# Earlier loads for the gate stage, three units ahead of its norm, and the last products on VectorE alone

## The chip, the core and the metric

The kernel runs on one core of a Trainium2 chip. The metric is the device time of one execution in microseconds (us). The core has a matrix engine, TensorE (PE), which multiplies 128 x 128 weights into 512 columns at a time; VectorE (DVE) and ScalarE (ACT) for elementwise work; GpSimd (POOL), which here adds squares and issues some transfers; and SyncE (SP), whose queue issues nearly all transfers between the device memory and the core's own memory. Each engine runs its own list of instructions in order and waits on semaphores of the others.

## The reference

One decoder layer on 1024 tokens of 2048 features in fp32:

```
hn = rmsnorm(h);  proj = hn @ w_in              # q, k, v, gate of two groups of 8 heads
mixed = [stick_breaking(..) * silu(g1), rmsnorm(differential(..)) * silu(g2)]
h = h + mixed @ w_out                           # 2048 x 2048
gate = sigmoid(rmsnorm(h) @ w_ple_gate)         # 2048 x 2048
h = h + gate * (p @ w_ple_proj)                 # p has 256 features
return rmsnorm(h)
```

The change lies in the last three lines and in the passage from the output projection to them.

## The kernel before

All tensors are held transposed: features on the 128 partitions, tokens along the free axis. The 1024 tokens are worked in two halves of 512; half 1 goes first through every stage, then half 0. The 2048 features are 16 channels of 128, and channels u and u + 8 belong to "unit" u. Every fp32 product is made of three matmuls on a high and a low part of each operand (high x high, high x low, low x high). ScalarE casts the high part and VectorE subtracts it to get the low part. For the gate these are `whi` (L151) and `wlo` (L152), made from the loaded `wraw` by `wprep`; `whi`, `wlo` and `wraw` each have two buffers.

*Output projection.* It runs as seven products of half the size (`prod`, matmuls L756 to L758) in two phases of eight units. In the second phase each unit loads four pieces of the residual (`hr`, L948) and adds them on VectorE (L972, L993, L996 and L939); the sums `hc` are put into the device buffer `h_d` by an accumulating transfer that GpSimd's queue issues (L744). The last unit's S4 product writes into a PSUM half whose other half `hc` of L939 reads.

*Gate stage.* `gate_loads` (L910 to L914) reads `h_d` back and makes `xh` and `xl`, the operands of the gate. `embedding` (L655 to L657) loads the 256 features of p (`praw`) and makes `ph` and `pl`, of which there is one copy. `plew` (L665 to L669) loads and splits a unit's projection weights (`pw`), and `ple` (L677 to L681) is 12 matmuls and a copy by ScalarE to `pls`. The tiles `praw`, `pw` and `hr` share the ring "xt" of four buffers, so a load waits until the tile four places earlier has been read. A gate unit, `unit` (L213 to L215), is 96 matmuls in four chunks of 24, one set of weights a chunk.

*Norm of the gate.* Its sum of squares is made beside the first units: `load_h` reads `h_d`, ScalarE squares (L105, L109), GpSimd adds (L110). The function `rstd` (L122 and L90 to L94) sums over the partitions on PE and takes the power; it needs two switches of ScalarE's function table and a third for the sigmoid. The norm scales the accumulator only after the matmuls: `gated` (L689 to L692) multiplies `acc` by `rstd`, takes the sigmoid, multiplies by `pls` and adds to h. For half 1, before: ple 0, ple 1, unit 0, unit 1 with the norm's matmul ahead of its last chunk, then for u from 2 to 7 ple u and unit u. Then follows half 0 in the same manner, with the final norm of half 1 beside it.

*The end.* The last unit is made in two quarters of 256 tokens (`tq`, L1108 to L1122). The sum of squares of the final norm closes behind each, and `final` (L623, L626) multiplies h by it and sends it out (L633): for the first quarter on GpSimd, for the second three pairs on GpSimd and the rest on VectorE.

*Order of the work.* PE's list is written out by hand over the whole kernel. Those of VectorE and ScalarE are written out by hand only in the output projection (`man2`) up to the first gate unit; behind that a planner, which simulates the engines, sorts them, and it sorts GpSimd's and SP's lists too.

Of the kernel before, what the change touches and what calls it, by code (L numbers as in the profile page):

```python
# [13 lines left out]
F32 = mybir.dt.float32  # L14
# [32 lines left out]
def _body(ctx, nc, tc, ap):  # L47
# [96 lines left out]
    def wprep(wsrc, pc, by_halves=False):  # L144
        raw = wp.tile([P, 2, 2, 2, P], F32, name="wraw", tag="wraw", bufs=2)
        hi = wp.tile([P, 2, 2, 2, P], F32R, name="whi", tag="whi")
        lo = wp.tile([P, 2, 2, 2, P], F32R, name="wlo", tag="wlo")

        def part(o):
            lastw[0] = nc.sync.dma_start(raw[:, o], wsrc[pc][:, o])  # L150
            A.copy(hi[:, o], raw[:, o])  # L151
            V.tensor_tensor(lo[:, o], raw[:, o], hi[:, o].bitcast(F32), op=ALU.subtract)  # L152

        part(slice(0, 1 if by_halves else 2))
        return hi, lo, partial(part, slice(1, 2))

    class Stream:
# [11 lines left out]
        def prep(self, by_halves=False):  # L169
            hi, lo, second = wprep(*self.todo.popleft(), by_halves=by_halves)  # L170
            self.ready.append((hi, lo))
            return second
# [261 lines left out]
    with tc.tile_pool(name="at", bufs=2) as at, tc.tile_pool(name="pz", bufs=2, space=PSUM) as pz:  # L434
# [217 lines left out]
        def embedding(half):  # L652
            for k in range(2):
                praw = ev.tile([P, HALF], F32, name="praw", tag="xt", bufs=4)
                nc.sync.dma_start(praw, ap["pT"][k * P:(k + 1) * P, half * HALF:half * HALF + HALF])  # L655
                A.copy(ph[:, k, :], praw)
                V.tensor_tensor(pl[:, k, :], praw, ph[:, k, :].bitcast(F32), op=ALU.subtract)  # L657
# [4 lines left out]

        def plew(half, u):
            wr = ev.tile([P, 2, 2, P], F32, name="pw", tag="xt", bufs=4)
            nc.sync.dma_start(wr, ap["w_pp"][u])  # L665
            wh = at.tile([P, 2, 2, P], F32R, name="pwh", tag="awh")
            wl = at.tile([P, 2, 2, P], F32R, name="pwl", tag="awl")
            A.copy(wh, wr)
            V.tensor_tensor(wl, wr, wh.bitcast(F32), op=ALU.subtract)  # L669
            plws[half, u] = wh, wl  # L670

        def ple(half, u):
            wh, wl = plws.pop((half, u))
            z = pz.tile([P, 2, HALF], F32, name="ple", tag="z")
            for c in range(2):
                for k in range(2):
                    T.matmul(z[:, c, :], wh[:, k, c, :], ph[:, k, :], start=k == 0, stop=False)  # L677
                    T.matmul(z[:, c, :], wh[:, k, c, :], pl[:, k, :], start=False, stop=False)
                    T.matmul(z[:, c, :], wl[:, k, c, :], ph[:, k, :], start=False, stop=k == 1)
            pls = pair("pls", "st")  # L680
            A.copy(pls, z)  # L681
            plss[half, u] = pls
# [259 lines left out]
        for ph in range(2):  # L942
            for u in range(8):
                last = ph == 1 and u == 7
                r = {}
                for e in ((1, u), (1, u + 8), (0, u), (0, u + 8)) if ph else ():
                    r[e] = ev.tile([P, HALF], F32, name="hr", tag="xt", bufs=4)
                    nc.sync.dma_start(r[e], half_d[e])  # L948
# [17 lines left out]
                if ph:  # L966
                    V.tensor_tensor(u2, u2, r[1, u + 8], op=ALU.add)

# [28 lines left out]
                if last:  # L997
                    p2()
                prev = u, ph, b, c, s1, u2
# [14 lines left out]
        while xq and len(xq) > 8:  # L1014
            xq.popleft()[1]()
# [26 lines left out]
        gated(1, 0, acc0, rstd)  # L1042
        gated(1, 1, acc1, rstd)
        for u in range(2, 8):
# [54 lines left out]
        for tq in range(2):  # L1099
# [13 lines left out]
            for c in range(2):  # L1113
# [8 lines left out]
                T.matmul(ms, ones, s, start=False, stop=c == 1)  # L1122
            with tc.issue_after(sgi.ins):
# [63 lines left out]
```

## Time and profile before

| | before |
|---|---|
| runs, us | 2513.76, 2515.78, 2515.96 |
| median, us | 2515.78 |
| the profiled execution's own time, us | 2510.27 |
| its span, us | 2508.5 |
| TensorE's mean granted clock, of 1 | 0.992 |
| TensorE busy | 2441.4 us, 97% |
| VectorE, ScalarE, GpSimd busy | 67%, 46%, 12% |

All times inside the profile count from the start of the span. The profiled execution is itself 2510.27 us, 1.8 us more than its span, and 5.5 us under the median of the three runs, so a sum made from its rows is a difference to be carried over to the median. In a row of the time order the columns are start, duration, engine, line, operation, what it writes and reads, tile shape, and in brackets the idle time of that engine ahead of it with what released it. A row of the windows gives the stretch, its length, the busy time of PE, weight loads, VectorE, ScalarE and GpSimd with instruction counts, then the granted clock of PE, the share of the transfer engines and the rate. The gate stage of half 1 runs from about 2083 us to 2287, that of half 0 to about 2500.

### The profile page before, as it was taken

Reading aid. Unit: us, or ns where it says so; the run is one execution under the profiler, and the core shown is the slowest. Engines: PE = TensorE matmul, PEld = TensorE weight load, DVE = VectorE, ACT = ScalarE, POOL = GpSimd, SP = SyncE. Lnnn points to the kernel's source line nnn. Section 1 sums busy time; section 2 is a strip of 40 time slices with the busy share of each in tenths; the row PEclk is TensorE's granted clock in tenths of the full one; section 3 lists DMA queues with packets and bytes.
Section 4 is the critical chain, followed back from the end, with each engine's and each line's share of the span. In section 5 each row is a group of like instructions: output and inputs, shape, how many; then the busy total and the mean of one; then the engine's idle time right before and its main releaser. Section 6 shows DMA issues by size and latency. Waiting matters only on the chain.

```text
span 2508.5 us, 31234 instructions
## 1 busy us (share of the span) xinstructions
PE 2441.4 (97%) x11626; PEld 2034.8 (81%) x11626; DVE 1668.4 (67%) x2677; ACT 1161.9 (46%) x1920; POOL 288.9 (12%) x281
## 2 busy tenths in 40 slices
PE   8999999999999999999999999999999998999996
PEld 7888888788887888888887888887787876888886
DVE  6554555777877888888876565667678673547555
ACT  6332333555556655555555333335523224637342
POOL 3000000300000000001111010101021114321112
PEclk9999999999999999999999999999999999999998
DMA  5333333633334333334443333435656786333433
GB/s 189 113 116 116 114 105 125 206 123 118 109 122 164 121 107 122 114 117 143 148 142 126 101 126 94 135 113 183 228 190 217 164 199 211 129 119 115 133 101 101
DMA packets 135415, 346.26 MB, mean 138 GB/s; under 512 B 14496, under 2 KB 18592, under 8 KB 135264
## 3 DMA queue, kind: packets, MB, share of 16 engines
q1 hardware_dynamic: 114096, 288.43, 35.6%
q0 software_dynamic: 21168, 55.85, 7.8%
q8 instruction: 91, 1.49, 0.2%
q14 instruction: 60, 0.49, 0.1%
HBM read 281.31 MB, written 71.30 MB: 141 GB/s over the span
## 4 chain that ended last, share of the span: by engine, by line
PE 87%; DVE 7%; DMA 2%; ACT 2%; issue 1%; SPq 0%; DVEq 0%; ACTq 0%
PE acc L213 20%; PE acc L214 20%; PE acc L215 20%; PE tp L345 2%; PE pbc L756 2%; PE pbc L758 2%; PE pbc L757 2%; DVE st L306 1%; PE z L286 1%; PE z L287 1%; PE av L378 1%; DVE wlo L152 1%; PE av L377 1%; PE av L376 1%; PE pa L758 1%
## 5 line engine op out<-in xcount | busy, mean ns | idle before, releaser
L213 PE MATMUL acc<-xh,whi 128*128 128x512 f32 x2464 | 981.4, 398 | 6.3 <-ACT xh L138 6.3
L214 PE MATMUL acc<-xl,whi 128*128 128x512 f32 x2464 | 963.9, 391 | 0.8 <-DVE xl L139 0.8
L215 PE MATMUL acc<-xh,wlo 128*128 128x512 f32 x2464 | 964.0, 391 | 0.0
L152 DVE TENSOR_TENSOR wlo<-wraw,whi 128x1024 fp32r<-128x1024 f32 (+1 forms) x317 | 398.8, 1258 | 374.5 <-ACT whi L151 369.2
L215 PEld LDWEIGHTS acc<-xh,wlo 128*128 128x128 f32 x2464 | 463.6, 188 | 101.1 <-DVE wlo L152 1.3
L151 ACT CAST whi<-wraw 128x1024 fp32r<-128x1024 f32 (+1 forms) x317 | 333.0, 1051 | 457.2 <-PE acc L214 397.0
L213 PEld LDWEIGHTS acc<-xh,whi 128*128 128x128 f32 x2464 | 464.8, 189 | 93.6 <-ACT xh L138 6.8
L214 PEld LDWEIGHTS acc<-xl,whi 128*128 128x128 f32 x2464 | 464.9, 189 | 88.3 <-DVE xl L139 2.3
L357 ACT CAST awh<-tp 128x256 fp32r<-128x256 f32 (+1 forms) x160 | 80.3, 502 | 180.9 <-PE tp L345 153.5
L358 DVE TENSOR_TENSOR awl<-tp,awh 128x256 fp32r<-128x256 f32 (+1 forms) x160 | 93.1, 582 | 97.9 <-ACT awh L357 96.7
L110 POOL TENSOR_TENSOR ssq<-ssq,sq 128x512 f32<-128x512 f32 x80 | 119.0, 1488 | 326.6 <-ACT sq L109 278.8
L314 ACT ACTIVATE et<-z,mx 128x512 f32<-128x512 f32 (+7 forms) x128 | 94.6, 739 | 53.6 <-DVE mx L311 52.7
L865 ACT CAST wpr<-T 128x512 fp32r<-128x512 f32 x64 | 39.2, 623 | 164.9 <-DVE T L822 164.0
L306 DVE TENSOR_TENSOR_SCAN st<-pt 128x511 f32<-128x511 f32 (+3 forms) x64 | 89.9, 1405 | 20.8 <-ACT pt L304 20.2
L311 DVE TENSOR_REDUCE mx<-z 128x1 f32<-128x512 f32 (+7 forms) x128 | 96.4, 753 | 1.2
L304 ACT ACTIVATE pt<-z 128x512 f32<-128x512 f32 (+3 forms) x64 | 41.6, 650 | 79.7 <-DVE z L293 79.7
L378 PE MATMUL av<-awl,v 128*128 128x256 f32 x256 | 73.4, 287 | 5.2 <-DVE awl L358 5.2
L376 PE MATMUL av<-awh,v 128*128 128x256 f32 x256 | 72.5, 283 | 0.7 <-ACT awh L357 0.7
L377 PE MATMUL av<-awh,v 128*128 128x256 f32 x256 | 72.3, 283 | 0.0
L286 PE MATMUL z<-k,q 128*128 128x512 f32 (+2 forms) x160 | 56.9, 360 | 4.5 <-ACT et L314 4.5
L322 DVE SCALAR_TENSOR_TENSOR et<-et,l 128x512 f32<-128x512 f32 (+3 forms) x64 | 53.0, 829 | 11.8 <-ACT et L321 11.8
L321 ACT ACTIVATE et<-et,l 128x512 f32<-128x512 f32 (+3 forms) x64 | 49.7, 777 | 17.6 <-DVE l L320 17.1
(309 smaller groups left out, 3627.8 us busy)
## 6 DMA issues: line engine op xcount, KB each, us to landing
wraw<-w_in SPq DMA_DIRECT2D x255, 512.0 KB, 3.6
wraw<-w_gate SPq DMA_DIRECT2D x64, 512.0 KB, 3.6
wraw<-w_out SPq DMA_DIRECT2D x56, 256.0 KB, 3.7
k_d<-k POOLq DMA_DIRECT2D x16, 512.0 KB, 3.9
v_d<-v POOLq DMA_DIRECT2D x16, 512.0 KB, 2.9
mixed_d<-sg SPq DMA_DIRECT2D x32, 256.0 KB, 3.1
k<-k_d POOLq DMA_DIRECT2D x16, 512.0 KB, 3.6
v<-v_d POOLq DMA_DIRECT2D x16, 512.0 KB, 4.4
```

The lines of the kernel that those rows point to most:

```text
L110: lastadd[0] = eng.tensor_tensor(self.acc, self.acc, s, op=ALU.add)
L151: A.copy(hi[:, o], raw[:, o])
L152: V.tensor_tensor(lo[:, o], raw[:, o], hi[:, o].bitcast(F32), op=ALU.subtract)
L213: T.matmul(acc[c], hi[:, k2, kh, c, :], xh, start=first, stop=False)
L214: T.matmul(acc[c], hi[:, k2, kh, c, :], xl, start=False, stop=False)
L215: T.matmul(acc[c], lo[:, k2, kh, c, :], xh, start=False, stop=last)
L306: V.tensor_tensor_scan(st[:, off + 1:nkey], pt[:, off:nkey - 1], pt[:, off:nkey - 1], initial=1.0, op0=ALU.mult, op1=ALU.bypass)
L311: V.reduce_max(mx, z[:, vw], axis=AX.X, negate=True)
L314: A.activation(et[:, vw], z[:, vw], AF.Exp, bias=mx[:, 0:1], accum_out=l)
L376: T.matmul(av, vv[:, 0, blk % 4, :], wh, start=blk == 2 * pr + 1, stop=False)
L377: T.matmul(av, vv[:, 1, blk % 4, :], wh, start=False, stop=False)
L378: T.matmul(av, vv[:, 0, blk % 4, :], wl, start=False, stop=last)
```

## The change

Line numbers in the texts are those of the kernel before. The change does the following.

1. The residual pieces `hr` are loaded in the order in which they are added.
2. The loads of p for half 1 get tiles of their own (the tags of the later `rstd` tiles) and are issued ahead of the last unit's residual; by the scheduler's order they stand far earlier in SP's list still. The loads of the projection weights of units 0 to 2 are issued within the last unit. The gate's first chunk is loaded before the A12 product of the last unit and split only after `rest_of(prev, True)`.
3. ple 0, 1 and 2, then units 0, 1 and 2 precede the use of the norm, whose matmul stands ahead of the last chunk of unit 2. From unit 3 on, ple u follows unit u on PE.
4. The residual of half 1 is read and squared one pair of channels at a time, one pair ahead of a chunk of units 0 to 2 (two at one chunk).
5. At the switch of halves, ple 7 of half 1 now comes behind unit 7, so that the embedding of half 0 is split between it and ple 0 of half 0.
6. At the end all products of `final` in half 0 are on VectorE; those of the first quarter are issued within the second quarter's chain.

The core of the diff:

```diff
-    def wprep(wsrc, pc, by_halves=False):
+    def wprep(wsrc, pc, by_halves=False, later=False):
...
+        def split(o):
+            A.copy(hi[:, o], raw[:, o])
+            V.tensor_tensor(lo[:, o], raw[:, o], hi[:, o].bitcast(F32), op=ALU.subtract)
         def part(o):
             lastw[0] = nc.sync.dma_start(raw[:, o], wsrc[pc][:, o])
+            if later:
+                return
+            split(o)
...
+        if later:
+            return hi, lo, partial(split, slice(0, 2))
...
-            self.prep()
+            return self.prep(later=True)
...
+        def embedding_load(half, tags):
             for k in range(2):
-                praw = ev.tile([P, HALF], F32, name="praw", tag="xt", bufs=4)
+                praw = ev.tile([P, HALF], F32, name="praw", tag=tags[k][0], bufs=tags[k][1])
                 nc.sync.dma_start(praw, ap["pT"][k * P:(k + 1) * P, half * HALF:half * HALF + HALF])
+                praws.append(praw)
+        def embedding():
+            for k in range(2):
+                praw = praws.pop(0)
...
+        def plew_load(half, u):
+            pws[half, u] = ev.tile([P, 2, 2, P], F32, name="pw", tag="xt", bufs=4)
+            nc.sync.dma_start(pws[half, u], ap["w_pp"][u])
...
-            pls = pair("pls", "st")
+            pls = pair("pls", "pt" if half == 1 and u == 2 else "st")
...
+                if last:
+                    embedding_load(1, (("rstd0", 1), ("rstd1", 1)))
                 r = {}
-                for e in ((1, u), (1, u + 8), (0, u), (0, u + 8)) if ph else ():
+                for e in ((1, u + 8), (1, u), (0, u + 8), (0, u)) if ph else ():
...
+                if last:
+                    plew_load(1, 0)
...
                 if last:
+                    gate0 = stream.gates()
                     p2()
+                    plew_load(1, 1)
+                    plew_load(1, 2)
...
-        embedding(1)
+        embedding()
         plew(1, 0)
-        stream.gates()
         rest_of(prev, True)
+        gate0()
         plew(1, 1)
         rest_of(prev, False)
...
         ple(1, 0)
+        plew(1, 2)
         ple(1, 1)
...
-        plew(1, 2)
+        ple(1, 2)
         s2 = SumSq(ev, "ssq")
+        ss1 = SumSq(ev, "rstd1")
...
+        def residual(u):
+            if u < 8:
+                load_h(1, u)
+            if u:
+                for c in range(2):
+                    ss1.add(h[1, u - 1 + 8 * c])
-        acc0 = unit(X, mid={2: xrest})
+        acc0 = unit(X, mid={2: xrest, 3: partial(residual, 0)})
+        za = pz.tile([P, 2, HALF], F32, name="za", tag="z")
+        acc1 = unit(X, acc=[za[:, 0, :], za[:, 1, :]], mid={i: partial(residual, i + 1) for i in range(4)})
         man2.__exit__(None, None, None)
-        ss1 = SumSq(ev, "rstd1")
-        for u in range(8):
-            load_h(1, u)
-            for c in range(2):
-                ss1.add(h[1, u + 8 * c])
-        za = pz.tile([P, 2, HALF], F32, name="za", tag="z")
+        zb = pz.tile([P, 2, HALF], F32, name="zb", tag="z")
...
-        acc1 = unit(X, acc=[za[:, 0, :], za[:, 1, :]], mid={3: lambda: rs.append(ss1.rstd(ev, "rstd0"))})
+        def norm1():
+            residual(8)
+            rs.append(ss1.rstd(ev, "rstd0"))
+        def more():
+            residual(6)
+            residual(7)
+        acc2 = unit(X, acc=[zb[:, 0, :], zb[:, 1, :]], mid={0: partial(residual, 5), 1: more, 3: norm1})
...
         gated(1, 0, acc0, rstd)
+        plew(1, 3)
         gated(1, 1, acc1, rstd)
-        for u in range(2, 8):
+        gated(1, 2, acc2, rstd)
+        for u in range(3, 8):
+            acc = unit(X)
             ple(1, u)
             if u < 7:
                 plew(1, u + 1)
             else:
-                embedding(0)
+                embedding_load(0, (("xt", 4), ("xt", 4)))
+                embedding()
                 plew(0, 0)
-            acc = unit(X)
-            for v in ((0, 1), (2, 3), (4,), (5,), (6,), (7,))[u - 2]:
+            for v in ((0, 1), (2, 3), (4, 5), (6,), (7,))[u - 3]:
...
+            if tq:
+                final(0, slice(0, Q), r2, range(8))
             with tc.issue_after(sgi.ins):
                 A.preload_act_table_set("natural_log_exp_and_others")
...
-            rstd_from(ms, 1.0 / NK, eps6, EPS, r2, r3)
-            if tq == 0:
-                final(0, ts, r2, range(8), eng=G)
-            else:
-                final(0, ts, r2, (0, 1, 2), eng=G)
-                final(0, ts, r2, (3, 7, 4, 5, 6))
+            with tc.high_priority(offset=400):
+                rstd_from(ms, 1.0 / NK, eps6, EPS, r2, r3)
+        final(0, ts, r2, range(8))
```

More of the change, by code (lines that the diff above doesn't have):

```diff
@@ L650, in load_h @@
                 h[half, u + 8 * c] = hc[c]
-        def embedding(half):
+        praws = []
+        def embedding_load(half, tags):
             for k in range(2):
-                praw = ev.tile([P, HALF], F32, name="praw", tag="xt", bufs=4)
+                praw = ev.tile([P, HALF], F32, name="praw", tag=tags[k][0], bufs=tags[k][1])
                 nc.sync.dma_start(praw, ap["pT"][k * P:(k + 1) * P, half * HALF:half * HALF + HALF])
+                praws.append(praw)
+        def embedding():
+            for k in range(2):
+                praw = praws.pop(0)
                 A.copy(ph[:, k, :], praw)
@@ L661, in _body @@
         plws = {}
+        pws = {}
+        def plew_load(half, u):
+            pws[half, u] = ev.tile([P, 2, 2, P], F32, name="pw", tag="xt", bufs=4)
+            nc.sync.dma_start(pws[half, u], ap["w_pp"][u])
         def plew(half, u):
-            wr = ev.tile([P, 2, 2, P], F32, name="pw", tag="xt", bufs=4)
-            nc.sync.dma_start(wr, ap["w_pp"][u])
+            if (half, u) not in pws:
+                plew_load(half, u)
+            wr = pws.pop((half, u))
             wh = at.tile([P, 2, 2, P], F32R, name="pwh", tag="awh")
@@ L1013, in _body @@
         xq.extend((slot[0], fn) for fn in gate_loads("S4"))
-        while xq and len(xq) > 8:
-            xq.popleft()[1]()
         last_ = [None, None]
```

6 lines of the change are left out of this document (2 added, 4 removed).

## The prediction

> **What bounds the kernel now.** I read four views in this order: the page's busy times and its chain, the waits of TensorE (PE) in the stretch the diff touches, the same stretch by windows, and single instructions in time order. First the page's two lines, then PE's waits from 2040 to 2150 us (total, times, longest), then a window with no wait in it (length, PE, weight loads, VectorE, ScalarE, GpSimd, granted clock, DMA share, GB/s).
>
> ```profile
> PE 2441.4 (97%) x11626; PEld 2034.8 (81%) x11626; DVE 1668.4 (67%) x2677; ACT 1161.9 (46%) x1920; POOL 288.9 (12%) x281
> ...
> PE 87%; DVE 7%; DMA 2%; ACT 2%; issue 1%; SPq 0%; DVEq 0%; ACTq 0%
> ```
> ```profile
> PE pbc L756 <- DVE hc L939: 5.8, 1, 5.8
> PE pbc L756 <- DVE hc L993: 1.8, 1, 1.8
> PE za L215 <- DVE wlo L152: 1.5, 1, 1.5
> PE za L213 <- ACT whi L151: 1.1, 1, 1.1
> ```
> ```profile
> 2150.00:2200.00 50.00, 50.00 (x223) 41.39 (x222) 23.54 (x23) 23.67 (x34) 17.81 (x12) 1.00 0.45 150
> ```
>
> PE is busy 97% of the span and carries 87% of the chain, so time is won or lost only where PE stands still or its clock falls. The changed kernel issues the same matmuls, and up to the last unit of the output projection all engines but the queues keep their order; I price that long part at nothing, since PE covers it. The window gives PE's pace: 50 us / 223 = 0.224 us a matmul, so 2.7 us for the 12 of one `ple`, 5.4 for a chunk of 24, 21.6 for a gate unit of 96. What is left is four places: the way into the gate stage, its first units, the switch of halves, and the end.
>
> **Place 1, the way into the gate.** Single instructions in time order (start, duration, tile, in brackets the idle time before and its releaser), one row of the chain, and one window:
>
> ```profile
> 2059.67 0.33 SPq L655 DMA_DIRECT2D praw<-pT  x1
> ...
> 2068.84 0.33 SPq L655 DMA_DIRECT2D praw<-pT  x1
> ...
> 2072.12 0.62 ACT L656 CAST ph<-praw 128x512 fp32r<-128x512 f32 x1 [5.65 <-DMA praw<-pT]
> ...
> 2075.00 0.62 ACT L668 CAST pwh<-pw 128x512 fp32r<-128x512 f32 x1 [2.26 <-DMA pw<-w_pp]
> ...
> 2076.60 1.23 DVE L152 TENSOR_TENSOR wlo<-wraw,whi 128x1024 fp32r<-128x1024 f32 x1 [0.25 <-ACT whi L151]
> 2077.74 0.68 DVE L939 TENSOR_TENSOR hc<-pbc,s 128x512 f32<-128x512 f32 x1
> ```
> ```profile
> 2078.48 0.79 PE L756 MATMUL pbc<-cS4h,wpr 128*128 128x512 f32 x1 [5.83 <-DVE hc L939]
> ```
> ```profile
> 2081.83 0.23 PE pbc L757
> ```
> ```profile
> 2075.00:2076.00 1.00, 0.00 (x0) 0.00 (x0) 0.35 (x1) 1.00 (x2) 0.00 (x0) 0.50 1.13 320
> ```
>
> PE stops at 2078.48 - 5.83 = 2072.65. The S4 product cannot start because `hc` stands on VectorE behind the splits of the embedding, of the first projection weights and of the gate's first chunk, and these wait for loads issued at 2059.67, 2068.84 and later. In the change the two `praw` loads take tiles of their own and go out far ahead, the projection loads move up into slots that the last unit's residual leaves, chunk 0 of the gate is loaded before the A12 product, and its split comes after `hc`. Then `hc` follows the A22 product at once: 2072.65 + 0.05 + 0.68 = 2073.4, against 2078.48: a gain of 5.0. With the stop goes the slow clock behind it: granted 0.50, 8 matmuls in 2081.83 - 2078.48 = 3.35 us where the pace makes 1.8, 1.5 more. The next thing that could be late is chunk 0's own split, VectorE's 1.23, but PE has the S4 product and three `ple` between, 48 matmuls or 10.8 us. The two early loads and the `plew` loads cost SP 0.33 us an issue at slots it passes anyway; PE does not wait on SP there. The 1.8 us wait on `hc` L993 stays: VectorE's order in front of it is the old one, and the other order of the residual loads only makes the tile it adds first come first. Bounds: none of the 6.5 (a load still late) to all.
>
> **Place 2, units 0 to 2.** ScalarE's waits grouped, single instructions, a chain row, and two windows:
>
> ```profile
> ACT sq L109 <- POOL ssq L110: 8.8, 10, 1.6
> ```
> ```profile
> 2113.72 0.64 ACT L109 ACTIVATE sq<-h 128x512 f32<-128x512 f32 x1 [0.74 <-POOL ssq L110]
> ...
> 2115.64 1.03 ACT L151 CAST whi<-wraw 128x1024 fp32r<-128x1024 f32 x1
> ...
> 2116.72 0.50 PE L213 MATMUL za<-xh,whi 128*128 128x512 f32 x1 [1.10 <-ACT whi L151]
> 2118.92 0.54 PE L215 MATMUL za<-xh,wlo 128*128 128x512 f32 x1 [1.47 <-DVE wlo L152]
> ```
> ```profile
> 2122.83 0.24 PE za L215
> ```
> ```profile
> 2068.00:2069.00 1.00, 0.00 (x0) 0.00 (x0) 0.93 (x3) 0.00 (x0) 0.00 (x0) 1.00 1.00 334
> 2119.00:2120.00 1.00, 1.00 (x3) 0.85 (x4) 0.58 (x1) 0.38 (x1) 1.00 (x1) 0.62 0.27 41
> ```
>
> Before, 16 squares stand in ScalarE's order and each waits for GpSimd's add of the one before (one square in 0.64 + 0.74 = 1.38 us). The cast `whi` of a chunk comes behind them and is late: 1.10 + 1.47 = 2.57 us, then 9 matmuls in 2122.83 - 2118.92 = 3.91 us where 2.0 are due: 1.9. In the changed order at most four squares stand between two casts: 4 x 1.38 = 5.5 plus 1.03 for the cast, in a chunk time of 5.4 with the next chunk already prepared, and mostly two: 2.8 + 1.0. So both go: a gain of 4.5. Bounds: 0, and a loss in the last rival.
>
> The cost stands at the norm. The chain row of the sum, then VectorE's end of it:
>
> ```profile
> 2131.24 0.86 PE ssps L122 x2
> ```
> ```profile
> 2137.53 0.69 DVE L94 SCALAR_TENSOR_TENSOR rstd<-ssq,rstd 128x512 f32<-128x512 f32 x1
> 2138.25 1.29 DVE L689 TENSOR_TENSOR gt<-acc,rstd 128x512 f32<-128x512 f32 x2
> ```
>
> From the sum's start T, `rstd` is there at T + 7.0 and VectorE has read the first accumulator at T + 7.7 (half of the pair: 2138.9 - 2131.24). PE has 0.5 for the sum and a chunk, T + 5.9, and then wants the accumulator that unit 0 holds. Before, a `ple` of 2.7 stood there and covered it; now all three stand ahead of the units, and unit 3 follows directly. PE waits 7.7 - 5.9 = 1.8. Six gated channels instead of four then queue on ScalarE and VectorE beside unit 3's splits; each channel is three products like those of the pair (0.65 each), so 11.7 us and four splits of 1.23 in 21.6 us: it fits, with little to spare at the third and fourth chunk: bounds 1.8 to 3.8, I take 1.8. An idle PE of 1.84 us alone left the clock at 1.00 (the window from 2068), so none is added for the clock.
>
> **Place 3, the switch of halves.** In time order:
>
> ```profile
> 2262.45 0.61 ACT L656 CAST ph<-praw 128x512 fp32r<-128x512 f32 x1
> ...
> 2263.49 1.00 ACT L681 COPY pls<-ple 128x1024 f32<-128x1024 f32 x1
> ...
> 2264.48 0.69 DVE L657 TENSOR_TENSOR pl<-praw,ph 128x512 fp32r<-128x512 f32 x1
> ...
> 2286.78 0.40 PE L679 MATMUL ple<-ph,pwl 128*128 128x512 f32 x1
> 2287.34 1.28 ACT L1073 ACT_TABLE_LOAD   x1
> ```
>
> The tiles `ph` and `pl` exist once. Before, `embedding(0)` overwrites them behind `ple(1,7)`, with gate unit 7 (21.6 us) as cover, at 2262.45. Now `ple(1,7)` comes behind unit 7 and `ple(0,0)` follows it on PE, so the rewriting lies open. PE's last matmul of unit 7 and `ple` together end near 2287.05, in either order. From there, in the changed order of ScalarE: the table load to 2288.62, `ph` 0 to 2289.25, a cast of weights (0.6), the copy of `pls` (1.00) to 2290.7, `ph` 1 to 2291.2; on VectorE `pl` 0 to 2290.0, its weights' remainder, two products of unit 7's gate that wait for that copy, `pl` 1 to 2292.6. PE can use one matmul at a time in between and runs freely from 2292.7; `ple(0,0)` ends near 2294.5 against 2287.05 + 2.7 = 2289.8: 4.7 lost. PE is idle for most of 5.6 us, and both earlier rows in which the idle time added up (0.50 from 2075, 0.62 at 2119 after 1.10 and 1.47) show the clock falling, at 1.5 and 1.9: I add 1.6, in all 6.3. Bounds: 4.5 (no clock, copies overlapped) to 7.5.
>
> [...]
>
> **Place 4, the end.** The group of GpSimd's last products (min/median/max ns), VectorE's instructions, and the transfers from 2487 to 2509 in 40 slices of 0.55 us:
>
> ```profile
> L626 POOL TENSOR_TENSOR h<-h,r x10: 1370/1441/1769, 2482.0 to 2498.9; 128x512 f32<-128x512 f32 x10
> ```
> ```profile
> 2475.48 0.42 DVE L1121 TENSOR_TENSOR sq<-h 128x256 f32<-128x256 f32 x1
> ...
> 2490.74 1.37 DVE L1121 TENSOR_TENSOR sq<-h 128x256 f32<-128x256 f32 x1
> ...
> 2495.30 0.42 DVE L94 SCALAR_TENSOR_TENSOR r<-r,r 128x256 f32<-128x256 f32 x1
> 2495.75 0.69 DVE L626 TENSOR_TENSOR h<-h,r 128x512 f32<-128x512 f32 x1
> ...
> 2499.17 2.95 DVE L626 TENSOR_TENSOR h<-h,r 128x512 f32<-128x512 f32 x3
> ```
> ```profile
> GB/s 359 339 330 350 337 276 278 28 344 104 179 298 0 0 0 0 0 0 35 350 121 344 103 13 343 121 11 318 333 345 343 276 257 326 149 26 0 0 0 0
> ```
>
> Beside GpSimd's products VectorE's own take longer (1.37 for a square that takes 0.42 alone, 0.98 for a product of 0.69). VectorE now does all: seven products of 0.69 and two of 0.42 for the first quarter come into the second quarter's chain from 2482.1, two of them behind the first `h`. Adding them with their neighbours at durations without GpSimd: 5 x 0.69 to 2485.6, `h` to 2486.0, 2 x 0.69 + 2 x 0.42 to 2488.2, square and product to 2489.0, sigmoid, product, `h` and square to 2490.6, against 2492.11: 1.5 earlier. The norm then ends at 2494.2 and the last nine at 2494.2 + 7 x 0.69 + 2 x 0.42 = 2499.9, against 2502.1. The output of that quarter, 2.1 MB at the 335 GB/s of the full slices, is 6.3 us from about 2496.4: 2502.7, and the last one's landing 2502.4 to 2503.4, against activity into the 36th slice, 2506.3. I take a gain of 3.5; bounds 2.5 (VectorE 0.15 slower an instruction) to 4.4.
>
> **The sum**, in the profiled execution: -5.0 - 1.5 - 2.6 - 1.9 = -11.0; +1.8; +6.3; -3.5: -6.4, so 2510.27 - 6.4 = 2503.9. The median of the runs lies 5.5 above the profiled one, and the change is carried over: 2515.78 - 6.4 = 2509.4. A change of 0.2% is 5.0 us, about what a measurement of this kernel can tell from none: faster is below 2510.7, slower above 2520.8.
>
> **Rivals.** *The clock holds at the switch*: 1.6 less, 2507.8; it needs the pieces of `ple(0,0)` to keep PE counted as busy, against which the two falls stand. *Unit 3 is late again*: a split of unit 3 stands behind the six channels, 2.0 more at Place 2, the other end of its bounds: 2511.4; for it, the close fit, against it, that four channels before left VectorE idle afterwards. *Place 1 keeps its stop*: a moved load waits for its slot until the residual adds are done, so `pwh`, and `pl` with it, still hold `hc` up: without the 6.5 it is 2515.9; for it, 2.26 us on `pw` in the old order, against it, that the changed order puts that load into the slot that opened at 2059.67. *The switch is hidden*: if ScalarE and VectorE get past the table load and the copy while PE still works, the 6.3 goes: 2503.1; against it, single `ph` and `pl`. *The slower end: squares hold the casts in units 0 to 2.* With a pair in every chunk, each square that waits for GpSimd or for its own `h` load pushes a cast; 1.3 us late at eight boundaries is 10.4, and the 4.5 of Place 2 are not won: -6.4 + 14.9 gives 2524.3. It decides from 5.0 + 6.4 = 11.4 us, that is with the 4.5 and some five late boundaries. For it speak the 8.8 us ScalarE spent waiting on GpSimd; against it, 3.8 us a pair and cast in 5.4 us of PE.
>
> **How the numbers follow.** As forecast 0.40 (own range 2505 to 2513.5, from the bounds of Places 2 to 4), clock holds 0.10, unit 3 late 0.16, Place 1 keeps its stop 0.12, switch hidden 0.08, squares 0.14. The range 2502 to 2517.5 leaves out the last case and a little at the fast end. Faster: 0.27 of the forecast's 0.40 (those below 2510.7), 0.09, 0.05 and 0.08, together 0.49; slower 0.13, the squares' case nearly whole; the same 0.38.
>
> **What would show it.** Right: no wait on `hc` L939 and a clock of 1.00 from the S4 product on; no wait on `whi` or `wlo` in units 0 to 2; a wait of about 2 us ahead of unit 3, released by VectorE's first `gt`; waits on `ph` and `pl` at the first `ple` of half 0, some 4.7 us with a fallen clock; no GpSimd work after the last gate unit, and the last square some 1.5 us sooner before its end. Wrong: a wait on `hc` L939 over 2 us, a `whi` wait at several chunks, a switch under 3 or over 8 us, or an end that does not shorten because the transfers, not VectorE, set it.

## The result and the profile after

The changed kernel takes 2507.83 us in the median of 7 executions (2506.39 to 2510.14); the kernel before, beside it, 2515.96 (2513.39 to 2518.77). The ratio is 0.9967 with a 95% interval of 0.9956 to 0.9979, so the change saves 8.1 us, 5.3 to 11.1 by the interval. The forecast was 2509.4, 6.4 us saved. The profiled execution took 2507.57 us, with a span of 2505.8.

Two lines of the page after, busy times and chain:

```profile
PE 2444.6 (98%) x11626; PEld 2036.3 (81%) x11626; DVE 1659.7 (66%) x2687; ACT 1158.0 (46%) x1920; POOL 274.2 (11%) x271
...
PE 86%; DVE 7%; ACT 3%; DMA 2%; issue 2%; POOL 0%; SPq 0%; DVEq 0%; ACTq 0%; POOLq 0%
```

PE's waits after, from 2000 us to the end (total, times, longest):

```profile
PE ple L698 <- ACT ph L670: 2.9, 1, 2.9
PE ssps L1167 <- DVE sq L1166: 2.6, 2, 1.5
PE pbc L777 <- DVE hc L1018: 1.8, 1, 1.8
PE acc L220 <- DVE gt L710: 1.5, 1, 1.5
PE ple L699 <- DVE pl L671: 0.8, 2, 0.6
PE pbc L777 <- DVE hc L960: 0.8, 1, 0.8
```

At the end, before, stood this one:

```profile
PE ssps L1122 <- DVE sq L1121: 4.7, 2, 3.5
```

The 5.8 us on `hc` is down to 0.8, the 4.7 at the quarters' sums to 2.6, the waits on `whi` and `wlo` are gone, the norm (1.5) and the switch of halves (2.9 and 0.8) have appeared, and the 1.8 on the other `hc` stands where it stood.

*Entry and first units* of the changed kernel, in time order:

```profile
2077.60 0.69 DVE L960 TENSOR_TENSOR hc<-pbc,s 128x512 f32<-128x512 f32 x1 [0.17 <-PE pbc L779]
```
```profile
2078.35 0.50 PE L777 MATMUL pbc<-cS4h,wpr 128*128 128x512 f32 x1 [0.79 <-DVE hc L960]
```
```profile
2121.98 1.05 ACT L150 CAST whi<-wraw 128x1024 fp32r<-128x1024 f32 x1 [3.34 <-PE za L221]
```

VectorE now waits for PE at `hc`, and ScalarE's cast waits for PE to release a weight buffer; before, PE waited for both.

*Norm and switch* after, in time order, then one window of the switch (granted clock third from the end):

```profile
2156.37 1.29 DVE L710 TENSOR_TENSOR gt<-acc,rstd 128x512 f32<-128x512 f32 x2
```
```profile
2157.21 0.47 PE L220 MATMUL acc<-xh,whi 128*128 128x512 f32 x1 [1.51 <-DVE gt L710]
...
2282.77 0.50 PE L698 MATMUL ple<-ph,pwh 128*128 128x512 f32 x1 [2.89 <-ACT ph L670]
...
2286.13 0.79 PE L699 MATMUL ple<-pl,pwh 128*128 128x512 f32 x1 [0.61 <-DVE pl L671]
...
2289.28 0.63 PE L700 MATMUL ple<-ph,pwl 128*128 128x512 f32 x1
```
```profile
2280.80 1.28 ACT L1118 ACT_TABLE_LOAD   x1
2282.10 0.62 ACT L670 CAST ph<-praw 128x512 fp32r<-128x512 f32 x1
```
```profile
2284.00:2285.00 1.00, 1.00 (x3) 0.28 (x1) 0.86 (x3) 0.66 (x2) 0.00 (x0) 0.50 0.30 61
```

*The end* after: VectorE's instructions, and the transfers from 2484 to 2506 us in 40 slices of 0.55.

```profile
2492.47 0.43 DVE L1166 TENSOR_TENSOR sq<-h 128x256 f32<-128x256 f32 x1
...
2495.56 0.42 DVE L94 SCALAR_TENSOR_TENSOR r<-r,r 128x256 f32<-128x256 f32 x1
2496.02 4.30 DVE L633 TENSOR_TENSOR h<-h,r 128x512 f32<-128x512 f32 x7
2500.24 0.87 DVE L630 SCALAR_TENSOR_TENSOR h<-h,gvec,r 128x256 f32<-128x256 f32 x2
```
```profile
GB/s 0 0 0 0 76 337 333 333 358 326 346 339 348 343 341 328 6 0 0 0 0 0 0 0 58 341 332 333 358 335 339 341 333 350 345 335 15 0 0 0
```

A product takes 0.61 us (4.30 / 7), the square 0.43, and the second quarter leaves in one run of full slices without the holes of before.

From the starts of PE's instructions, four stretches can be laid side by side: *entry*, from the last matmul but one of the last unit's A12 product to the first `ple`; *half 1*, to the first norm matmul of half 0; *half 0*, to the last matmul of the gate; *end*, to the end of the span. In us:

| profile | up to the entry | entry | half 1 | half 0 | end | entry to end |
|---|---|---|---|---|---|---|
| before | 2067.2 | 15.6 | 204.2 | 199.0 | 22.5 | 441.3 |
| before, second profile (same_again) | 2070.4 | 17.1 | 202.0 | 199.0 | 22.5 | 440.5 |
| changed | 2072.2 | 9.0 | 208.5 | 199.2 | 16.9 | 433.6 |
| changed, second profile (changed_again) | 2067.2 | 9.1 | 208.3 | 200.2 | 17.3 | 434.9 |
| switch_and_norm | 2072.0 | 9.1 | 200.8 | 199.0 | 16.8 | 425.7 |
| entry_tuned | 2069.2 | 7.7 | 200.8 | 199.0 | 16.8 | 424.4 |

The last column falls by 5.6 to 7.7 us with the change. The two first profiles differ by only 2508.5 - 2505.8 = 2.7 us, because in the changed one PE reached the entry 4.9 us later, in a part whose PE order is the same. The next experiment asks whether that belongs to the change.

### The profile page after: what moved, and what is told of

Same layout as the page of the kernel before. It is cut to its first block, busy times and chain, and to the rows that moved or that the text cites. A ratio compares the mean times of both kernels' runs of the same rounds, so it can differ in the third digit from the quotient of the medians.

```text
span 2505.8 us, 31225 instructions
## 1 busy us (share of the span) xinstructions
PE 2444.6 (98%) x11626; PEld 2036.3 (81%) x11626; DVE 1659.7 (66%) x2687; ACT 1158.0 (46%) x1920; POOL 274.2 (11%) x271
## 4 chain that ended last, share of the span: by engine, by line
PE 86%; DVE 7%; ACT 3%; DMA 2%; issue 2%; POOL 0%; SPq 0%; DVEq 0%; ACTq 0%; POOLq 0%
PE acc L220 20%; PE acc L221 20%; PE acc L222 20%; PE tp L352 2%; PE pbc L777 2%; PE pbc L779 2%; PE pbc L778 2%; DVE st L313 1%; PE z L293 1%; PE z L294 1%; PE av L385 1%; PE av L384 1%; PE av L383 1%; DVE wlo L151 1%; PE pa L779 1%
## 5 line engine op out<-in xcount | busy, mean ns | idle before, releaser
L220 PE MATMUL acc<-xh,whi 128*128 128x512 f32 x2432 | 969.7, 399 | 8.4 <-ACT xh L138 6.9
L221 PE MATMUL acc<-xl,whi 128*128 128x512 f32 x2432 | 952.4, 392 | 0.5 <-DVE xl L139 0.5
L222 PE MATMUL acc<-xh,wlo 128*128 128x512 f32 x2432 | 952.4, 392 | 0.0
L222 PEld LDWEIGHTS acc<-xh,wlo 128*128 128x128 f32 x2432 | 458.4, 188 | 100.1 <-DVE wlo L151 1.3
L220 PEld LDWEIGHTS acc<-xh,whi 128*128 128x128 f32 x2432 | 458.9, 189 | 95.0 <-ACT xh L138 7.3
L221 PEld LDWEIGHTS acc<-xl,whi 128*128 128x128 f32 x2432 | 459.4, 189 | 86.4 <-DVE xl L139 1.7
L294 PE MATMUL z<-kl,qz 128*128 128x512 f32 (+2 forms) x160 | 57.5, 359 | 0.0
```

Of the source, the lines that this page charges most:

```text
L220: T.matmul(acc[c], hi[:, k2, kh, c, :], xh, start=first, stop=False)
L221: T.matmul(acc[c], hi[:, k2, kh, c, :], xl, start=False, stop=False)
L222: T.matmul(acc[c], lo[:, k2, kh, c, :], xh, start=False, stop=last)
```

## The experiments

All medians of the kernel before lie between 2514.9 and 2516.7 us; each ratio is against it on the same chip. The ratios' intervals reach about 0.1 to 0.17% to each side, some 2.5 to 4 us, so a smaller difference between two changed kernels rests on their profiles alone.

**The kernel before, again, and the changed kernel, again.** No edit.

> The kernel before once more, unchanged. In the two profiled executions at hand the changed kernel runs 5.0 us late by the last unit of the output projection (PE's product ahead of the A22 one starts at 2074.58 us, not 2069.69), though PE's order up to there is the same; behind it the changed kernel gains 7.7. Theory one: those 5.0 us differ from execution to execution whatever the kernel, and the profiled execution of before happened to have little of them. Then this run's time is within 0.1% of the kernel before, and its profile has that product anywhere between 2069 and 2076 us, with the same 5.8 us wait on hc L939 behind it. Theory two: the 5.0 us come with the change (the early loads of p, the order of the residual loads). Then this profile has the product at 2069 to 2071 again.

> The changed kernel once more, beside the kernel before on the same chip. Theory: 0.997 again, within the interval of the first measurement (0.9956 to 0.9979); in the profile the stretch from the last unit's A22 product to the end is within 1 us of the first profile's 431.2, while the stretch before it may differ by a few us. Rival (the changed kernel is really slower in the stretch before, and its first 7 runs were lucky): 0.9985 or more.

Measured: before again, 1.0001 (0.9988 to 1.0015), with PE at the A22 product at 2072.82, inside the forecast span, and 6.3 us of wait behind it where 5.8 was expected. (The 2069.69 and 2074.58 of the expectation are starts of the A22 product too, not of the one ahead of it.) The changed kernel again, 2507.85 us, 0.9974 (0.9963 to 0.9985). A row of each second profile in time order, the A22 product, first of before, then of the changed kernel:

```profile
2072.82 0.47 PE L756 MATMUL pbc<-cA,wpr 128*128 128x512 f32 x1 [1.81 <-DVE hc L993]
```
```profile
2069.60 0.47 PE L777 MATMUL pbc<-cA,wpr 128*128 128x512 f32 x1 [1.81 <-DVE hc L1018]
```

Each kernel has now been seen earlier and later there (2069.7 and 2072.8; 2074.6 and 2069.6), the changed one by as much as the 4.9 us. The medians show no loss ahead of the entry either: less 1.8 us and less the last column of the table, they give an estimate of 2072.9 and 2072.6 for the kernel before, 2072.4 and 2071.2 for the changed one. So the 4.9 us are put down to the two executions; that a small part of them comes with the change is not excluded. A sum made from one profile is therefore good for the stretch in which the edit lies, and the difference of two single executions is not a measurement. "From A22 to the end" moved from 431.2 to 2502.1 - 2069.6 = 432.5, 1.3 rather than the 1 expected.

**The end alone**, on the kernel before:

```diff
+            if tq:
+                final(0, slice(0, Q), r2, range(8))
...
-            rstd_from(ms, 1.0 / NK, eps6, EPS, r2, r3)
-            if tq == 0: ...   # finals on GpSimd
+            with tc.high_priority(offset=400):
+                rstd_from(ms, 1.0 / NK, eps6, EPS, r2, r3)
+        final(0, ts, r2, range(8))
```

> The kernel before with the end of the change alone: all last products on VectorE, those of the first quarter inside the second quarter's chain. Theory one (beside GpSimd's products VectorE's own take two to three times as long, and without them the chain closes sooner and the transfers follow one another without gaps): in the profile the stretch from the last matmul of the gate to the end of the span is 5 us shorter than before, and the time 5.2 us lower, 2510, a ratio of 0.998. Rival (the end is set by how fast 2.1 MB leave, at 335 GB/s, so that the order of the products matters little): 2 us or less.

Measured: 2508.71 us against 2515.44, 0.9977 (0.9966 to 0.9987): 5.8 us by the ratio. In its profile the end is 16.8 us long, as in the changed kernel, against 22.5. The first theory holds. This part is worth 5.6 us by itself and does not need the others. The edit moves the products to VectorE and changes their place in its order at once; the two were not run apart.

**p loaded late**, on the changed kernel:

```diff
-                if last:
-                    embedding_load(1, (("rstd0", 1), ("rstd1", 1)))
...
                 if last:
+                    embedding_load(1, (("xt", 4), ("xt", 4)))
                     plew_load(1, 0)
```

> The changed kernel with the two loads of p put back into the ring that the residual uses, behind the last unit's residual and ahead of the projection weights; everything else stays. Theory one (the long wait of before hangs on the slots: the second half of p waits for a slot until the last residual add on VectorE, some 2 us before the A22 product ends, and pl with hc behind it waits for its landing): a wait of 3.5 to 5 us on hc L960 ahead of the S4 product with the clock at 0.50 behind it, the stretch from the A22 product to the first ple 11 to 13 us in place of 6.6, the time 4.5 to 6 us above the changed kernel. Rival (the projection weights' early loads are what counts): the wait stays under 2 us.

Measured: 2513.48 us, 0.9987 (0.9976 to 0.9999), 5.6 us above the changed kernel's median on the same chip, 3.3 by the two ratios, whose intervals overlap. From the A22 product to the first `ple` it is 12.7 us (2074.64 to 2087.36), as expected. SP's queue, one of its waits, ScalarE, VectorE and PE of this profile:

```profile
2073.80 0.33 SPq L664 DMA_DIRECT2D praw<-pT  x1
2075.12 3.97 SPq L681 DMA_DIRECT2D pw<-w_pp  x4
```
```profile
SPq L681 <- DVE s L1020: 0.9, 1, 0.9
```
```profile
2081.05 0.62 ACT L689 CAST pwh<-pw 128x512 fp32r<-128x512 f32 x1 [3.04 <-DMA pw<-w_pp]
```
```profile
2082.30 0.68 DVE L960 TENSOR_TENSOR hc<-pbc,s 128x512 f32<-128x512 f32 x1
```
```profile
PE pbc L777 <- DVE hc L960: 4.1, 1, 4.1
```

The wait is back, by a longer chain than expected. The second half of p waits for its slot until 2073.80. The weights' load, which the two loads of p have pushed two places on in the ring, then waits for a slot of its own, the one that the add `s` of L1020 frees, and goes out at 2075.12; `hc` waits behind the split of those weights. So late loads cause the stop, and in this run the weights' load is the last link. What a late load of p alone would cost was not run, since in one ring the one pushes the other back. Of the 6.1 us that this stretch is longer than the changed kernel's 6.6, the wait makes 3.3 (4.1 for 0.8) and the slow clock behind it 1.5 (matmuls 0.43 us apart, where the pace is 0.22); the other 1.4 is a fall of the clock already in the A22 product (again 0.43 us apart, from 2076.2), behind the 1.8 us wait that both kernels have.

**The split moved ahead again**, on the changed kernel:

```diff
+        gate0()
         rest_of(prev, True)
-        gate0()
```

> The changed kernel with one line moved back: the gate's first chunk is split ahead of hc of L960 (L939 before), as in the kernel before, while every load stays early. Theory one (the 5.8 us wait of before came from loads that were late, and the order of the split on VectorE is worth its own 1.2 us only): the wait on hc L960 grows from 0.8 to about 2.0 us, the time by 1 us at most. Rival (the order is what counts): the wait is 4 us or more, the clock falls to 0.50 behind it, and the time rises by 4 to 6 us.

Measured: in the profile the wait on `hc` L960 stays at 0.8.

```profile
2078.70 1.22 DVE L151 TENSOR_TENSOR wlo<-wraw,whi 128x1024 fp32r<-128x1024 f32 x1
2080.22 0.69 DVE L960 TENSOR_TENSOR hc<-pbc,s 128x512 f32<-128x512 f32 x1 [0.31 <-PE pbc L779]
```
```profile
2079.00:2080.00 1.00, 1.00 (x3) 0.37 (x2) 0.92 (x1) 1.00 (x3) 0.00 (x0) 0.50 1.03 238
```

Both theories expected some growth; there is none, because the clock fell to 0.50 (2078 to 2080 us) in this execution after the earlier 1.8 us wait, and the A22 product ended later. At full speed the split would be done at 2079.92 against an `hc` that could start about 1.3 us sooner, so up to 1 us is hidden here. The rival is out: the order is not what held PE. The time, 2511.08 us, 0.9987 (0.9975 to 0.9999), is 3.2 above the changed kernel, of which the profile from the entry on shows 1.0, about the price of that fall; the rest is not explained, and the intervals overlap.

**The squares in a row**, on the changed kernel:

```diff
-        acc0 = unit(X, mid={2: xrest, 3: partial(residual, 0)})
+        acc0 = unit(X, mid={2: xrest})
+        man2.__exit__(None, None, None)
+        for u in range(8):
+            load_h(1, u)
+            for c in range(2):
+                ss1.add(h[1, u + 8 * c])
...
-        acc1 = unit(X, acc=[...], mid={i: partial(residual, i + 1) for i in range(4)})
-        man2.__exit__(None, None, None)
+        acc1 = unit(X, acc=[...])
...
-        acc2 = unit(X, acc=[...], mid={0: partial(residual, 5), 1: more, 3: norm1})
+        acc2 = unit(X, acc=[...], mid={3: norm1})
```

> The changed kernel with the residual's eight pairs read and squared in one go from unit 1 on, sorted by the planner as in the kernel before, but with the norm still at the last chunk of unit 2. Theory one (late casts in the first units come from squares that stand in a row on ScalarE and go at GpSimd's pace): two waits on whi and wlo of 1 to 1.5 us are back in units 1 and 2 with a fallen clock, the time is 4.5 us above the changed kernel, 2512. Rival (the third unit ahead of the norm leaves room for the planner to spread them, and it is this unit and not the single pairs that took the waits away): no such wait, the same time as the changed kernel.

Measured: 2511.01 us, 0.9983 (0.9973 to 0.9994), 3.2 us above by the medians, with overlapping intervals. Two waits of its profile:

```profile
PE za L222 <- DVE wlo L151: 1.5, 1, 1.5
PE za L220 <- ACT whi L150: 0.3, 1, 0.3
```

The late cast is back, the clock held at 1.00 this time (2120 to 2126 us), and half 1 is 210.5 us against 208.5: 2.0, under half of the 4.5. So the single pairs, not the third unit, took the waits away. The edit also ends the hand-written order of VectorE and ScalarE (`man2`) one unit sooner, so it is the pairs in that order that are shown to do it. What they save depends on whether the clock falls.

**The residual's order of loads**, back to the old one:

```diff
-                for e in ((1, u + 8), (1, u), (0, u + 8), (0, u)) if ph else ():
+                for e in ((1, u), (1, u + 8), (0, u), (0, u + 8)) if ph else ():
```

> The changed kernel with the residual pieces loaded in the old order. Theory one (they land long before use in either order, so the order is worth nothing on PE): the same PE waits and the same time as the changed kernel, within 1.5 us. Rival: the early part of the kernel, the second phase of the output projection above all, shortens or lengthens by 2 us or more, with new waits on u or hc in it.

Measured: 2509.01 us, 0.9973 (0.9962 to 0.9985), the same waits behind 2040 us, 1.8 and 0.8 on `hc` among them. That part of the change is worth nothing that can be seen.

**The switch covered**, on the changed kernel:

```diff
         for u in range(3, 8):
+            if u == 6:
+                plew(1, 7)
+            if u == 7:
+                ple(1, 7)
+                embedding_load(0, (("xt", 4), ("xt", 4)))
+                embedding()
+                plew(0, 0)
             acc = unit(X)
-            ple(1, u)
...
+            if u < 7:
+                ple(1, u)
...
```

> The changed kernel with ple(1,7) put back ahead of unit 7, so that the embedding of half 0 is split beside that unit's matmuls. Theory one (the switch is an open stall of PE, and its price adds to the rest): the waits on ph and pl at the first ple of half 0 (2.9 and 0.8 us) and the slow clock behind them go, in the profile 7 to 8 us from the end of the gate stage of half 1 to the first gate unit of half 0; against the kernel before -8.1 - 7.5 = -15.6, near 2500 us, a ratio of 0.994. Rival (unit 7 then has too much on ScalarE and VectorE: embedding, xh and xl of half 0, gate splits): a wait on whi, wlo or xh inside unit 7 or unit 0 of half 0 takes part of it, and the time stays above 2504.

Measured: 2500.89 us, 0.9946 (0.9930 to 0.9961). All of PE's waits in its profile from 2040 us on:

```profile
PE ssps L1171 <- DVE sq L1170: 2.6, 2, 1.5
PE pbc L777 <- DVE hc L1018: 1.8, 1, 1.8
PE acc L220 <- DVE gt L710: 1.5, 1, 1.5
PE pbc L777 <- DVE hc L960: 0.8, 1, 0.8
```

The waits on `ph` and `pl` are gone and none came in their place; half 1 is 201.2 us, 7.3 less, and the time 6.9 less than the changed kernel's by the medians, 5.3 by the ratios.

**The norm sooner**, and **both**:

```diff
-        acc2 = unit(X, acc=[...], mid={0: partial(residual, 5), 1: more, 3: norm1})
+        acc2 = unit(X, acc=[...], mid={0: partial(residual, 5), 1: more, 2: norm1})
```

> The changed kernel with the norm's matmul ahead of chunk 2 of unit 2 in place of chunk 3; its last add on GpSimd is done some 4 us before that in the profile. Theory one (unit 3 waits 1.5 us because the chain from the sum to the first gated product takes 7.2 us and PE has only 5.9): with 5.4 us more of PE work between, the wait on gt ahead of unit 3 goes, and the time is 1.5 us lower than the changed kernel, about 2506 us, which the timing alone would hardly show; the profile shows it. Rival (the six gated channels are the bound, not the chain's latency): the wait goes, but a wait on wlo of 1 to 2 us shows up in unit 3, and the time does not move.

> Both edits together. Theory one: the two prices add, -8.1 - 7.5 - 1.5 = -17.1 against the kernel before, near 2499 us, ratio 0.9932, and PE has no wait over 1 us between the S4 product and the last unit's quarters. Rival: once the stalls are gone VectorE or ScalarE come to be late inside the gate units, and the sum is 3 us or more short.

Measured: alone 2508.0 us, 0.9971 (0.9961 to 0.9980); both 2499.97, 0.9943 (0.9928 to 0.9957). The wait on `gt` is gone, and in unit 3 of the first profile stands

```profile
2169.70 0.50 PE L222 MATMUL acc<-xh,wlo 128*128 128x512 f32 x1 [0.61 <-DVE wlo L151]
```

Half 1 is 0.8 us shorter, with the switch covered 0.4. Both theories had a share: the chain's latency made the wait, and once it is gone the six gated channels hold up one split. Together they save 15.1 us by the medians, 14.3 by the ratio, where 17.1 was expected; the norm's 1.5 us, which came to 0.4, are 1.1 of what is missing, and the rest lies within the interval. PE has no wait over 1 us in the gate stage.

**The switch filled**, on the changed kernel: 12 more matmuls whose result is not used.

```diff
             else:
+                fill = pp.tile([P, HALF], F32, name="fill", tag="t")
+                for i in range(12):
+                    T.matmul(fill, onesr, qzs[0][:, 0, :], start=i == 0, stop=i == 11)
                 embedding_load(0, (("xt", 4), ("xt", 4)))
```

> The changed kernel with 12 matmuls put between ple(1,7) and ple(0,0) of half 0 whose result nobody reads (2.7 us of PE work on operands that are always there); it only fills PE's wait for ph. It tells the stall apart from the clock that falls behind it. Theory one (the switch costs 7.7: 3.7 of waiting and piecemeal work that stays, and 2.5 to 3 of slow clock that comes from the idle time): the clock stays at 1.00 through the switch, ple(0,0) ends near 2287.5 on the changed kernel's time scale in place of 2289.7, and the time is 2 to 3 us below the changed kernel. Rival (the clock falls from the pieces that follow too, or the fill itself delays ple(0,0)): clock at 0.50 again or a later first ple, time the same or higher.

Measured: 2505.91 us, 0.9966 (0.9956 to 0.9976), not told apart from the changed kernel. PE in time order, and two windows (the first was at 0.50 in the changed kernel):

```profile
2279.41 2.96 PE L1096 MATMUL fill<-qz,onesr 128*128 128x512 f32 x12
2282.34 0.50 PE L698 MATMUL ple<-ph,pwh 128*128 128x512 f32 x1
...
2284.29 0.49 PE L698 MATMUL ple<-ph,pwh 128*128 128x512 f32 x1 [0.49 <-ACT ph L670]
2285.70 0.50 PE L699 MATMUL ple<-pl,pwh 128*128 128x512 f32 x1 [0.92 <-DVE pl L671]
```
```profile
2284.00:2285.00 1.00, 0.49 (x1) 0.19 (x1) 1.00 (x3) 0.23 (x1) 0.00 (x0) 1.00 0.60 207
2287.00:2288.00 1.00, 1.00 (x4) 0.81 (x3) 0.00 (x0) 1.00 (x2) 0.00 (x0) 0.50 0.70 225
```

My theory falls in the main: the long wait is filled, but the clock comes to 0.50 all the same, behind the pieces of 0.5 and 0.9 us that follow. It falls later: the windows show 1.00 from 2284 to 2285 and 0.50 from 2287 to 2288, where the changed kernel was at 0.50 from 2283.2 to 2290.0, and half 1 is 0.8 us shorter. So filling one hole bought back a part of the slow clock and little time; only covering the whole rewriting won it all.

**The entry tuned**, on switch_and_norm:

```diff
-            for _ in range(2):
+            late = ph == 1 and u == 7
+            for _ in range(0 if late and nm == "S3" else 4 if late and nm == "A12" else 2):
...
+        rest_of(prev, True)
         embedding()
         plew(1, 0)
-        rest_of(prev, True)
         gate0()
```

> switch_and_norm with two more edits at the entry of the gate stage: in the last unit the splits of the gate's operands that stood between the S3 product and hc L1018 come one product later, and rest_of(prev, True) stands ahead of the embedding's splits. Theory one (the remaining 1.8 and 0.8 us waits on hc come from VectorE's queue ahead of it): both go, the stretch from the A22 product's wait to the first ple is 5.5 us with a clock of 1.00, and the time is 1.5 to 3 us below switch_and_norm, 2497.5, ratio 0.993. Rival (VectorE is full there, and what is moved behind delays ple(1,0) or the gate's first chunk): a wait on pl, pwl or wlo of 1 to 2 us in its place, the same time.

Measured: 2499.35 us, 0.9932 (0.9916 to 0.9949), the fastest kernel of this study, 17.1 us below before by the ratio. PE's waits from 2040 us on:

```profile
PE ssps L1172 <- DVE sq L1171: 2.6, 2, 1.5
PE pbc L777 <- DVE hc L961: 0.8, 1, 0.8
PE acc L222 <- DVE wlo L151: 0.6, 1, 0.6
PE pbc L777 <- DVE hc L1019: 0.5, 1, 0.5
```

The 1.8 us wait is down to 0.5 and the entry from 9.1 to 7.7 us. The other `hc` keeps its 0.8, which is VectorE's 0.69 between two dependent products and no queue; there the first theory asked too much. Against switch_and_norm the gain is 0.6 us by the medians, 2.8 by the ratios (on two chips) and 1.3 in the profile, below what the timing resolves.

## Why the prediction was right, and where its terms were off

The time lies 1.6 us under the forecast and inside the likeliest case's own range. The four places were the right ones. That the total fits so well is in part luck: the terms are off by up to 2.7 us, some too large and some too small. Their sizes, by the stretches above:

| place | forecast | measured | by |
|---|---|---|---|
| 1, entry | -6.5 | -6.5 to -8.0 | entry 15.6 and 17.1 to 9.1 |
| 2, first units | -4.5 | -1.8 to -4.3 | half 1 of three profiles of the old order, less a clean 200.2 |
| 2, norm | +1.8 | +1.5 waited, 0.4 to 0.8 net | the wait; half 1 with the norm sooner |
| 3, switch | +6.3 | +7.3 | half 1 with the switch covered |
| 4, end | -3.5 | -5.1 to -5.6 | end 22.5 to 17.3 and 16.9; alone 5.6 |

The clean 200.2 is switch_and_norm's half 1 without its 0.6 us wait; the third profile of the old order is that of end_alone, with 204.5.

*Place 1* came out as worked. Its cause was told with one part too many: the gate's first chunk was named among the splits that hold `hc` up, and the order of that split is worth 1 us at most.

*Place 2* was taken at its upper end, because both waits and the fall of the clock were counted as certain. In the second profile of before PE did not wait for `whi`, and the 1.47 us on `wlo` alone left the clock whole:

```profile
2120.70 0.50 PE L213 MATMUL za<-xh,whi 128*128 128x512 f32 x1
2122.91 0.50 PE L215 MATMUL za<-xh,wlo 128*128 128x512 f32 x1 [1.47 <-DVE wlo L152]
```
```profile
2123.00:2124.00 1.00, 1.00 (x5) 0.83 (x6) 0.59 (x1) 0.37 (x1) 1.00 (x1) 1.00 0.10 12
```

*Place 2, norm.* The wait was 1.5, not 1.8, and moving it away shows the other end of the bounds too: one split is 0.6 us late.

*Place 3.* The stall and the fallen clock came as forecast. The term that was mis-sized is the start: the table load was set 0.3 us behind PE's last matmul of `ple(1,7)`; in the profile it starts at 2280.80, PE having run dry at 2282.77 - 2.89 = 2279.88. That is 0.9 us, since ScalarE was still busy with half 0's operands and with the last sigmoid of unit 7. With it the last wait, on `pl`, ended 2286.13 - 2279.88 = 6.2 us behind PE's last matmul, where 5.6 was forecast.

*Place 4* is the largest error that all profiles show. From the last matmul of the gate the norm closed 2495.72 - 2486.05 = 9.7 us later before and 2495.98 - 2488.94 = 7.0 after: 2.6 gained where 1.5 was forecast. Of the 1.1 between them, 0.6 is the products: in a row they took 0.61 us and not the 0.69 of the single one that was quoted, and the chain carried seven of them. The other 0.5 was not forecast: PE's last sum, first of before, then of the changed kernel,

```profile
2492.16 1.22 PE L1122 MATMUL ssps<-sq,onesr 128*128 128x256 f32 x2 [3.52 <-DVE sq L1121]
```
```profile
2492.95 0.70 PE L1167 MATMUL ssps<-sq,onesr 128*128 128x256 f32 x2 [1.46 <-DVE sq L1166]
```

ran at a granted clock of 0.50 before and of 1.00 after. It is not sure to be won: in the changed kernel's second profile the sum took 1.22 us again, as at the 0.50 of before, and its end is 17.3. The transfers then ended 7.8 us behind the norm (2503.8, where the GB/s row ends, less 2496.0), 0.4 less than the short end of the forecast's 8.2 to 9.2.

Of the rivals, none came true. The squares did not hold the casts; the slot did not hold the loads. "The clock holds at the switch" is out, with 0.50 from 2283.2 to 2290.0; that its 2507.8 lies nearest the measured time is a coincidence of the end's 2.1 us more and the switch's 1.0.

## What to carry to other kernels

When an engine's hand-written order puts work with an outside dependence (here the splits of just loaded p and weights) ahead of an instruction that PE waits for, give the load a tile of its own and an early place in its queue; the order itself then hardly matters. A single-copy tile that is rewritten between two users costs the whole rewriting if the users become neighbours on PE: here 7.3 of the 15 us that the rest had won, got back by moving 12 matmuls. And a sum over places is safer than the difference of two profiled executions, which here showed 2.7 us where the kernels differ by 8.

## What the runs showed of the hardware that was not expected

Behind short waits of PE the granted clock fell in some executions and held in others. The 1.47 us wait on `wlo` was followed by a granted clock of 0.62 and then 0.50 in the first profile of before, where a wait of 1.10 us had ended some 2 us before, and by 0.68 (2123 to 2124 us) in end_alone, where one of 1.4 did. Without that wait, in the second profile of before, and behind 0.3 us in squares_in_a_row, it left the clock at 1.00. The 1.8 us wait on `hc`, always alone, left it at 1.00 in both profiles of before and both of the changed kernel, and the matmuls behind it 0.23 us apart in residual_old_order; it was followed by 0.50 in split_ahead (2078 to 2080) and switch_covered (2079 to 2080), and by matmuls 0.43 us apart in p_loaded_late. At the switch of switch_filled, pieces of 0.2, 0.5 and 0.9 us were enough for 0.50. The two first profiles show eight falls to 0.50 ahead of the end; they lasted 3.4 us (5 of them) or 6.8 us (3). Among them the 5.8 us wait on `hc` and the 2.9 us one at the switch both went with 6.8, the 1.47 us one on `wlo` with 3.4. The waits ahead of the falls at `wlo`, behind the 1.8 us and at the switch were 2.9 us at the longest. What sets off a fall is not shown.

VectorE beside GpSimd is not slowed evenly. Before, a square of 256 columns took 0.42 us alone and 1.37 beside GpSimd's products, which take 1.37 at the least and 1.44 in the median themselves; after, without GpSimd, 0.43. A product of VectorE that reads one of its operands from PE's accumulator (`acq`) kept its time in their midst:

```profile
2487.81 0.41 DVE L1116 TENSOR_TENSOR gt<-acq,rstd 128x256 f32<-128x256 f32 x1
```

Why the one was slowed and the other not, no run here shows. The end of this kernel is 5.6 us shorter with the work on one engine.
